# The values of a gated linear attention by seven block products of 512 columns, and weight tiles placed by the step at which they come free

## The chip, the cores and the metric

The kernel runs on one core of a Trainium2 chip. The metric is the device time of one execution in microseconds (us). Before the change three runs gave 1188.12, 1188.62 and 1190.53 us, so the median is 1188.62.

## What is computed

Three residual layers on x of 512 tokens by 1024 features, all in fp32: a gated feed-forward network (FFN) with weight 0.5, a mixer, and a second FFN with weight 0.5; then a last norm.

```python
def swiglu(x, w_gu, w_down):                      # D_FF = 2816
    g, u = jnp.split(x @ w_gu, 2, axis=-1)
    return (jax.nn.silu(g) * u) @ w_down

def hybrid_mixer(h, w_in, ...):                   # 4 heads, dk 128, dv 256, CHUNK 64
    z = h @ w_in
    cb, cc, cu, q, k, v, g_lr, r, ga, gb = jnp.split(z, SPLIT_POINTS, axis=-1)
    y_conv = (cb * causal_short_conv(cc * cu, conv_w)) @ w_out_conv
    log_a = jax.nn.log_sigmoid(g_lr @ gate_w_up + gate_b) / GATE_TAU
    o = gla_chunked(q, k, v, log_a)
    o = o * lax.rsqrt(jnp.mean(o * o, axis=-1, keepdims=True) + EPS)
    y_gla = (o * gla_norm_g * jax.nn.silu(r)) @ w_out_gla
    merged = jax.nn.sigmoid(ga) * y_conv + jax.nn.sigmoid(gb) * y_gla
    return merged @ w_o

def reference(x, ...):
    x = x + 0.5 * swiglu(rmsnorm(x, norm_ffn1_g), ffn1_w_gu, ffn1_w_down)
    x = x + hybrid_mixer(rmsnorm(x, norm_mix_g), w_in, ...)
    x = x + 0.5 * swiglu(rmsnorm(x, norm_ffn2_g), ffn2_w_gu, ffn2_w_down)
    return rmsnorm(x, final_norm_g)
```

For each head and each chunk of 64 tokens, gla_chunked works out scores of q and k under decays, their product with the values v, and a state of 128 x 256 that is carried from chunk to chunk.

## The kernel before, in words

**Three matmuls for each product.** Weights come from HBM as tiles of 128 x 1024 fp32 (512 KB, name f) through SP's DMA queue (line 285). ScalarE (ACT) casts a tile to its high part wh (line 312), VectorE (DVE) forms the low part wl as the difference of tile and cast (line 313). Activations are kept as such pairs too (name op). A product is then wh x op-high + wl x op-high + wh x op-low: three matmuls on TensorE (PE) of 512 or 256 columns each, summed in a bank of 128 x 512 fp32 (names mm and aux).

**Sets of seven products.** Most of the wide products run as sets: a 2 x 2 block product by seven block products instead of eight, named m1, p2, q6, p5, q7, p4, p3. In the sets of 256 columns (line 501) weights are the stationary operand. A set loads four tiles a11, a12, a21, a22. A DVE sum forms s3 = a11 + a21 (line 299), and accumulating DMAs on GpSimd's (POOL's) queue form the other sums in place (line 290): a21 += a22 with the sum s3, a11 += a21 after the cast for m1, a12 += a11 after the cast for p2. The activations' sums are made by a class Operands (make; on DVE, lines 540 to 561, 600 and 737). The FFN's down product begins with two sets in the other layout ("wide", line 799, function run_wide): there the activations are stationary and 512 columns of weights move; each product consists of two half sets of 12 matmuls on two banks.

**What sets the order.** PLAN lists the weight tiles in the order of use and STEPS the casts (a tile alone, or a set and its product). The class Weights goes through STEPS two casts ahead of TensorE: each take issues what is due, that is loads (those of a set six steps ahead of its m1), sums (three steps ahead), the cast and the difference. Each engine works through its instructions in the order in which the program issues them. The f tiles come from a pool that hands out ten buffers in a ring: a new tile waits until the tile that was issued ten tiles ago has been read for the last time.

**The mixer.** First come q and k of heads 0 and 1 (mm_group, line 361), with the low-rank gates beside them. Then come the values, in two halves of 512 columns for heads 0 and 1, and 2 and 3 (v_half, which calls mm_wide, lines 378 to 380): for each pair of weight tiles all four blocks of 128 tokens, on four banks. Between the halves stand q and k of heads 2 and 3 (mm_single, line 347). Behind them come twelve sets (MSETS) for the gates ga and gb, the convolution (conv, cb) and r. The heads' chain (gates, decays, scale, scores, state, output, squares) runs within this order: for head 0 in the first half of the values and the singles, for head 1 from the last single to set 0, for heads 2 and 3 by hooks in sets 1 to 5. The outputs O of heads 0 and 1 are first kept in tiles that the convolution needs and are copied to their own tile after set 0 (move). The values are made from the activations before the norm's factor of each token, so k is multiplied by the factor's square (row2).

## Time and profile before

| | |
|---|---|
| runs | 1188.12, 1188.62, 1190.53 us |
| the profiled execution, its whole time | 1188.83 us |
| its span in the profile | 1187.1 us |
| share of time: PE, DVE, ACT, POOL | 99%, 72%, 53%, 9% |
| HBM | 124.55 MB read, 8.39 MB written |

The span reaches from the first to the last instruction of the profiled execution. Times in rows are in us; a row of a group names line, engine, operation, the tile written and the tiles read, and the count. "mean" durations are from an instruction's start to its end; neighbours on an engine overlap, so the pace of a stage is read from start to start. "Idle before" is time in which the engine had nothing running ahead of the group's instructions, with the engine that ended most of it.

The casts, differences and sums of all stages together:

```profile
L312 ACT CAST wh<-f 128x1024 fp32r<-128x1024 f32 (+1 forms) x335 | 349.5, 1046 | 406.0 <-PE mm L501 226.9
L313 DVE TENSOR_TENSOR wl<-f,wh 128x1024 fp32r<-128x1024 f32 (+1 forms) x335 | 405.9, 1216 | 169.4 <-ACT wh L312 160.0
L501 PE MATMUL mm<-op,wh 128*128 128x256 f32 x3584 | 470.3, 284 | 1.0 <-ACT tp L509 0.9
```

### The profile page before, as it was taken

The page shows a single profiled execution, that of the slowest core. Times are in us where ns is not written, and L with a number is a line of the kernel's source. Part 1 is how long each engine was busy: PE and PEld are TensorE (multiplying, and loading weights), DVE is VectorE, ACT ScalarE, POOL GpSimd, SP SyncE. Part 2 cuts the span into 40 slices and gives each one's busy share as a digit, 9 for nine tenths or more (in the row PEclk, how much of TensorE's full clock was granted, in tenths as well). Part 3 has the DMA queues.
Part 4 walks back from the last instruction along what each step waited for, and adds up shares of the span by engine and source line. Part 5 has one row for each costly group of instructions (what it writes and reads, how often), then busy time and mean ns, then how long its engine had stood idle before and what let it go on. Part 6 is the DMA issues. An engine that isn't in the chain of part 4 may idle for free. (4 is left out here: it accounts for less than half of the span.)

```text
span 1187.1 us, 19179 instructions
## 1 busy us (share of the span) xinstructions
PE 1176.9 (99%) x7818; PEld 1084.1 (91%) x7818; DVE 858.5 (72%) x1016; ACT 629.8 (53%) x784; POOL 111.8 (9%) x147
## 2 busy tenths in 40 slices
PE   9999999999999999999999999999999999999997
PEld 7899999988888889999999998998889999998876
DVE  7986665896578765768577687685598666579955
ACT  6554544675345465656554576544355454556443
POOL 0011111101010001101111100100001111001100
PEclk9999999999999999999999999999999999999999
DMA  9387777678532335867887766542538777757721
GB/s 350 80 219 187 179 187 186 150 198 209 196 112 83 89 71 156 203 192 205 219 230 176 194 195 186 142 125 80 177 76 212 167 186 174 191 142 184 173 87 71
DMA packets 61736, 197.10 MB, mean 166 GB/s; under 512 B 6768, under 2 KB 13040, under 8 KB 61648
## 3 DMA queue, kind: packets, MB, share of 16 engines
q1 hardware_dynamic: 39088, 126.37, 30.4%
q0 software_dynamic: 17920, 65.02, 29.8%
q10 hardware_dynamic: 4640, 4.49, 1.2%
q8 instruction: 61, 1.00, 0.3%
q14 instruction: 27, 0.22, 0.1%
HBM read 124.55 MB, written 8.39 MB: 112 GB/s over the span
## 5 line engine op out<-in xcount | busy, mean ns | idle before, releaser
L312 ACT CAST wh<-f 128x1024 fp32r<-128x1024 f32 (+1 forms) x335 | 349.5, 1046 | 406.0 <-PE mm L501 226.9
L313 DVE TENSOR_TENSOR wl<-f,wh 128x1024 fp32r<-128x1024 f32 (+1 forms) x335 | 405.9, 1216 | 169.4 <-ACT wh L312 160.0
L501 PE MATMUL mm<-op,wh 128*128 128x256 f32 x3584 | 470.3, 284 | 1.0 <-ACT tp L509 0.9
L501 PEld LDWEIGHTS mm<-op,wh 128*128 128x128 f32 x3584 | 447.4, 192 | 2.6 <-ACT tp L509 1.3
L501 PE MATMUL mm<-op,wl 128*128 128x256 f32 x1792 | 251.5, 283 | 0.0
L501 PEld LDWEIGHTS mm<-op,wl 128*128 128x128 f32 x1792 | 231.3, 192 | 0.1
L290 POOL DMA_DIRECT2D f<-f x120 | 103.6, 869 | 927.2 <-DVE wl L313 504.6
L347 PE MATMUL mm<-op,wh 128*128 128x512 f32 x384 | 91.8, 391 | 0.0
L347 PEld LDWEIGHTS mm<-op,wh 128*128 128x128 f32 x384 | 71.9, 188 | 14.8
L799 PE MATMUL mm<-wh,op 128*128 128x512 f32 x320 | 79.2, 390 | 0.1
L799 PEld LDWEIGHTS mm<-wh,op 128*128 128x128 f32 x320 | 59.9, 188 | 12.9 <-ACT wh L312 0.6
L361 PE MATMUL mm<-op,wh 128*128 128x512 f32 x256 | 63.8, 391 | 0.3 <-DVE op L412 0.3
L361 PEld LDWEIGHTS mm<-op,wh 128*128 128x128 f32 x256 | 47.8, 188 | 10.7 <-ACT acc L421 0.5
L299 DVE TENSOR_TENSOR f<-f,f 128x1024 f32<-128x1024 f32 x40 | 48.9, 1221 | 0.7
L347 PE MATMUL mm<-op,wl 128*128 128x512 f32 x192 | 47.4, 389 | 0.0
L347 PEld LDWEIGHTS mm<-op,wl 128*128 128x128 f32 x192 | 36.0, 188 | 7.5
L799 PE MATMUL mm<-wl,op 128*128 128x512 f32 x160 | 42.8, 389 | 0.0
L509 ACT COPY tp<-mm 128x512 f32<-128x512 f32 x68 | 39.7, 583 | 0.0
L799 PEld LDWEIGHTS mm<-wl,op 128*128 128x128 f32 x160 | 30.0, 188 | 6.2
L361 PE MATMUL mm<-op,wl 128*128 128x512 f32 x128 | 34.4, 391 | 0.0
L600 DVE TENSOR_TENSOR op<-hidw,op 128x1024 fp32r<-128x1024 f32 x28 | 33.9, 1218 | 0.1
L415 ACT ACTIVATE op<-X,vec 128x512 fp32r<-128x512 f32 x23 | 16.6, 720 | 31.8 <-DVE X L852 24.3
(273 smaller groups left out, 1151.6 us busy)
## 6 DMA issues: line engine op xcount, KB each, us to landing
f<-wts SPq DMA_DIRECT2D x219, 512.0 KB, 4.4
f<-f POOLq DMA_DIRECT2D x120, 512.0 KB, 4.9
X<-xT SPq DMA_DIRECT2D x8, 256.0 KB, 5.2
xs<-X POOLq DMA_DIRECT2D x8, 256.0 KB, 2.3
ga<-tp ACTq DMA_DIRECT2D x8, 256.0 KB, 2.9
gb<-tp ACTq DMA_DIRECT2D x8, 256.0 KB, 5.0
tp<-ga SPq DMA_DIRECT2D x8, 256.0 KB, 5.2
y<-tp SPq DMA_DIRECT2D x7, 256.0 KB, 2.0
```

What stands on the lines that cost most here:

```text
L290: return nc.gpsimd.dma_start(out_, a, accum_op=ALU.add).ins
L299: nc.vector.tensor_tensor(out=s3, in0=a11, in1=a21, op=ALU.add)
L312: self.cast = nc.scalar.copy(h[:, :w], raw[:, :w]).ins
L313: nc.vector.tensor_tensor(out=l[:, :w], in0=raw[:, :w], in1=h[:, :w].bitcast(F32), op=ALU.subtract)
L347: nc.tensor.matmul(o, w[:, i * P : (i + 1) * P], a[k], start=j == k == 0, stop=j == 2 and k == kt - 1)
L361: nc.tensor.matmul(o[c], w[:, s : s + P], a[k], start=k == 0 and j == 0, stop=k == kt - 1 and j == 2)
L415: nc.scalar.activation(xh[k], x[k], AF.Copy, scale=g)
L501: nc.tensor.matmul(to, ww[:, s], aa[:, t], start=fresh and k == 0 and e == 0 and j == 0, stop=k == 3 and j == 2, skip_group_check=True)
L509: nc.scalar.copy(v, o)
L600: nc.vector.tensor_tensor(out=lv, in0=v, in1=hv.bitcast(F32), op=ALU.subtract)
L799: nc.tensor.matmul(o[t], aa[:, s], ww[:, i * 512 : (i + 1) * 512], start=fresh and j == k == 0, stop=j == 2 and k == 3, skip_group_check=True)
```

## The change

1. **Values.** mm_wide and the list wide are gone. The four singles (q and k of heads 2 and 3) come directly after the first group. Behind them the values of all heads run as one wide set of 1024 columns, by the body of run_wide, which becomes a function (natural_set). The operands are those of the sets behind it (xo). The seven results are combined into the values' tiles vt by v_done. Since the operands now carry the norm's factor, k takes it once.
2. **The heads' chain.** Gates, decays and scale of head 0 are issued between the singles, its scores after the first product m1 of the values. All the rest, for four heads, hangs at sets 0 to 8 (the table chain). MSETS has another order at its start. O is written to its own tile from the start.
3. **Load tiles.** The f tiles get ten slots of one buffer each. A load names the step at which its tile is read for the last time (until), and takes the slot whose present tile is freed at the earliest step. A set asks for a21, a11, a22, the sum's tile and a12 in that order; before, it was a11, a12, a21, a22 and the sum's tile. A first set behind a wide set loads eight steps ahead of its m1 instead of six.

```diff
-MSETS = [("ga", 0), ("gb", 0), ("conv", 0), ("ga", 1), ("conv", 1), ("gb", 1), ("conv", 2),
+MSETS = [("ga", 0), ("gb", 0), ("ga", 1), ("conv", 0), ("gb", 1), ("conv", 1), ("conv", 2),
          ("conv", 3), ("cb", 0), ("cb", 1), ("r", 0), ("r", 1)]
...
+SLOTS = 10
 SEQ = ("m1", "p5", "q6", "p2", "q7", "p3", "p4")
...
     units(group("w_in", KD, (QO, KO, QO + P, KO + P)))
-    units(wide("w_in", KD, VO))
     for h in (2, 3):
         units(single("w_in", KD, QO + h * P))
         units(single("w_in", KD, KO + h * P))
-    units(wide("w_in", KD, VO + 512))
+    wide_sets("w_in", 1, VO)
...
                 if p == "m1":
-                    self.loads.setdefault(max(lo, i - first), []).append(n)
+                    after = STEPS[i - 1][1] is not None and PLAN[STEPS[i - 1][0]][4] > HW
+                    wait = PLAN[n][4] == HW and after
+                    self.loads.setdefault(max(lo, i - (8 if wait else first)), []).append(n)
...
+        def slot(self, until):
+
+            i = min(range(SLOTS), key=lambda j: self.until[j])
+            self.until[i] = until
+            cnt[0] += 1
+            return pools["f"].tile([P, 1024], F32, tag=f"f{i}", name=f"f{cnt[0]}")
...
+        def load_set(self, n):
+
+            a = {p: STEPS.index((n, p)) for p in SEQ}
+            for i in range(self.issued, a["m1"]):
+                if STEPS[i][1] is None and STEPS[i][0] not in self.raw:
+                    self.raw[STEPS[i][0]] = self.dma(STEPS[i][0], i)
+            a21 = self.dma(n + 2, max(a["p5"], a["m1"] + 3))
+            a11 = self.dma(n, a["p2"] + 3)
+            a22 = self.dma(n + 3, a["p4"])
+            s3 = self.slot(a["q7"])
+            a12 = self.dma(n + 1, a["p3"])
+            self.raw[n] = [a11, a12, a21, a22, s3]
...
-                self.raw[n] = [self.dma(n + i) for i in range(4)] + [tile_of("f", [P, 1024])]
+                self.load_set(n)
...
+    def natural_set(ops, banks, done, ahead=1):
+
+        used = {"a"}
+        for at, p in enumerate(SEQ):
+            for q in SEQ[at : at + ahead + 1]:
+                ops.make(q)
...
-        mul(row2, row, row)
...
+        def v_done(p, o):
+            for t in range(2):
+                if p == "m1":
+                    nc.scalar.copy(A[t], o[t])
+                elif p == "p2":
+                    nc.scalar.copy(vt[0][t], o[t])
+                elif p == "p5":
+                    nc.scalar.copy(vt[1][2 + t], o[t])
+                elif p == "q6":
+                    nc.scalar.copy(vt[0][2 + t], o[t])
+                elif p == "q7":
+                    v = vt[1][2 + t]
+                    nc.vector.scalar_tensor_tensor(out=v, in0=o[t], scalar=-1.0, in1=v,
+                                                   op0=ALU.mult, op1=ALU.subtract)
+                elif p == "p3":
+                    v = vt[0][2 + t]
+                    nc.vector.tensor_tensor(out=v, in0=o[t], in1=v, op=ALU.add)
+                else:
+                    nc.scalar.activation(vt[1][t], o[t], AF.Copy, scale=-1.0)
+            if p == "m1":
+                scores(0)
+
+        steps = [lambda: gates(0), decays, lambda: scale(0)]
+        for h in range(2, HEADS):
+            for c, evac in ((QO, evac_q), (KO, evac_k)):
+                o = mm_single("w_in", KD, c + h * P, xh, xl)
+                if steps:
+                    steps.pop(0)()
+                if c == QO:
+                    xo.make("p2" if h == 3 else "m1")
+                elif h == 2:
+                    xo.sum("p5")
+                evac(h, o)
+        A = [MM(), MM()]
+        natural_set(xo, {"a": A, "b": [MM(), MM()], "c": [MM(), MM()]}, v_done)
...
+        chain = [(0, "q6", state, 0), (0, "q7", output, 0), (0, "p3", squares, 0),
+                 (1, "q6", gates, 1), (1, "q7", None, 1), (1, "p4", scale, 1),
+                 (2, "q6", scores, 1), (2, "q7", state, 1), (2, "p4", output, 1),
+                 (3, "q6", squares, 1), (3, "q7", gates, 2), (3, "p3", None, 2),
+                 (4, "q6", scale, 2), (4, "p3", scores, 2), (5, "q6", state, 2),
+                 (5, "p4", output, 2), (5, "p3", squares, 2), (6, "q6", gates, 3),
+                 (6, "q7", None, 3), (6, "p4", scale, 3), (7, "q6", scores, 3),
+                 (7, "q7", state, 3), (7, "p4", output, 3), (8, "q6", squares, 3)]
+        for n, p, f, h in chain:
+            hooks[n, p] = [(lambda f=f, h=h: f(h)) if f else decays]
```

Below, the rows name an engine's instructions in the order of its program: line, operation, the tile written and the tiles read, and the shape; a number behind a name tells tiles of one name apart.

TensorE in the values, before: the first rows of a half (wh_3646 and wl_3647 are the parts of its first pair of weight tiles, op_3345 and op_3346 those of an activation tile, mm_3754 to mm_3757 the banks of the four blocks of tokens).

```order
L378 MATMUL mm_3754<-wh_3646,op_3345 128x512
L379 MATMUL mm_3754<-wl_3647,op_3345 128x512
L380 MATMUL mm_3754<-wh_3646,op_3346 128x512
L378 MATMUL mm_3755<-wh_3646,op_3345 128x512
L379 MATMUL mm_3755<-wl_3647,op_3345 128x512
L380 MATMUL mm_3755<-wh_3646,op_3346 128x512
```

The same engine after the change, where product m1 passes from its first half set (wh_3857, wl_3858) to its second (wh_3905, wl_3906); op_3813 and op_3814 are the operand's two parts. Left out are rows that read like the pair above them.

```order
L625 MATMUL mm_3937<-wl_3858,op_3813 128x512
L625 MATMUL mm_3938<-wl_3858,op_3813 128x512
L625 MATMUL mm_3937<-wh_3905,op_3813 128x512
L625 MATMUL mm_3938<-wh_3905,op_3813 128x512
...
L625 MATMUL mm_3937<-wh_3905,op_3814 128x512
L625 MATMUL mm_3938<-wh_3905,op_3814 128x512
...
L625 MATMUL mm_3937<-wl_3906,op_3813 128x512
L625 MATMUL mm_3938<-wl_3906,op_3813 128x512
```

Before, a pair's difference was needed by the pair's second matmul and was used on four banks (48 matmuls for every two pairs). Now a half set has 12 matmuls on two banks, and its difference is needed by the ninth.

VectorE ahead of the values' second half set, after the change: wl_3906 is the difference named above, the rows with g, y and sm scale head 0, L1043 works on the residual X, L1019 evacuates the last but one single product.

```order
L476 TENSOR_TENSOR y_3465<-g_566_3765,y_3465 128x512
L476 TENSOR_TENSOR g_565_3764<-g_565_3764,y_3465 128x4x64
L476 TENSOR_TENSOR g_566_3765<-g_565_3764,y_3465 128x256
L476 TENSOR_TENSOR g_566_3765<-y_3465,sm 128x256
L476 TENSOR_TENSOR y_3465<-g_564_3763,y_3465 128x512
L476 TENSOR_TENSOR g_565_3764<-g_566_3765,sm 128x4x64
L476 TENSOR_TENSOR g_567_3766<-g_566_3765,sm 128x4x64
L476 TENSOR_TENSOR g_567_3766<-y_3465,sm 128x4x64
L476 TENSOR_TENSOR d_3768<-sm 128x4
L1043 SCALAR_TENSOR_TENSOR X<-X,vec,row_3716 128x512 x4
L1019 SCALAR_TENSOR_TENSOR qk_3470<-mm_3856,row_3716 128x512
L332 TENSOR_TENSOR wl_3906<-f_3599,wh_3905 128x1024
```

Before, this scaling stood within the first half of the values, ahead of a difference that only the singles used:

```order
L475 TENSOR_TENSOR y_3465<-g_555_3747,y_3465 128x512
L475 TENSOR_TENSOR g_556_3748<-g_557_3749,sm 128x4x64
L475 TENSOR_TENSOR g_558_3750<-g_557_3749,sm 128x4x64
L475 TENSOR_TENSOR g_558_3750<-y_3465,sm 128x4x64
L313 TENSOR_TENSOR wl_3875<-f_3758,wh_3874 128x1024
L561 TENSOR_TENSOR op_4117<-X,op_4116 128x1024
L540 TENSOR_TENSOR X<-X 128x4x256
```

VectorE in the up product of the second FFN, before: the sum f_10088 of a set (line 299; f_10080 is the set's a11) and the differences behind it, up to the one that reads f_10080 for the set's m1.

```order
L299 TENSOR_TENSOR f_10088<-f_10080,f_10084 128x1024
L710 SCALAR_TENSOR_TENSOR hidw_8771<-mm_9889,tp_9980 128x2x256
L313 TENSOR_TENSOR wl_10185<-f_9848,wh_10184 128x1024
L313 TENSOR_TENSOR wl_10215<-f_9852,wh_10214 128x1024
L715 TENSOR_TENSOR tp_10242<-mm_10050,tp_10048 128x512
L313 TENSOR_TENSOR wl_10253<-f_9856,wh_10252 128x1024
L475 TENSOR_TENSOR hidw_8771<-tp_10119,tp_10242 128x2x256
L313 TENSOR_TENSOR wl_10284<-f_10080,wh_10283 128x1024
```

The same place after the change (the set's a11 is f_10092):

```order
L318 TENSOR_TENSOR f_10096<-f_10092,f_10090 128x1024
L332 TENSOR_TENSOR wl_10133<-f_9865,wh_10132 128x1024
L730 SCALAR_TENSOR_TENSOR tp_10129<-mm_10060,tp_10127 128x512
L332 TENSOR_TENSOR wl_10164<-f_9633,wh_10163 128x1024
L734 SCALAR_TENSOR_TENSOR hidw_8781<-mm_9899,tp_9990 128x2x256
L332 TENSOR_TENSOR wl_10195<-f_9860,wh_10194 128x1024
L332 TENSOR_TENSOR wl_10225<-f_9858,wh_10224 128x1024
L739 TENSOR_TENSOR tp_10252<-mm_10060,tp_10058 128x512
L332 TENSOR_TENSOR wl_10263<-f_9864,wh_10262 128x1024
L476 TENSOR_TENSOR hidw_8781<-tp_10129,tp_10252 128x2x256
L332 TENSOR_TENSOR wl_10294<-f_10092,wh_10293 128x1024
```

Three differences stood between the sum and the set's first one; now there are five.

More of the change, by code (lines that the diff above doesn't have):

```diff
@@ L604, in get @@
             return self.parts[p]
+    def natural_set(ops, banks, done, ahead=1):
[3 more added lines that the diff above has]
+                ops.make(q)
+            n = {"m1": "b", "p2": "a", "q6": "b", "p5": "c", "q7": "b", "p4": "b", "p3": "c"}[p]
+            fresh = n not in used
+            used.add(n)
+            o = banks[n]
+            bh, bl = ops.get(p)
+            for u in range(2):
+                h, l = W.take()
+                for j, (ww, aa) in enumerate(((h, bh), (h, bl), (l, bh))):
+                    for i in range(2):
+                        k = 2 * u + i
+                        for t in range(2):
+                            s = slice(k * HW + t * P, k * HW + (t + 1) * P)
+                            nc.tensor.matmul(o[t], aa[:, s], ww[:, i * 512 : (i + 1) * 512],
+                                             start=fresh and j == k == 0,
+                                             stop=j == 2 and k == 3, skip_group_check=True)
+            done(p, o)
     def run_sets(make, ahead=2, hooks={}):
```

118 lines of the change are left out of this document (21 added, 97 removed).

## Prediction

> **What bounds the kernel now.** I read the page's engine table first, then TensorE's waits, then windows of the stages that the change touches.
>
> ```profile
> span 1187.1 us, 19179 instructions
> PE 1176.9 (99%) x7818; PEld 1084.1 (91%) x7818; DVE 858.5 (72%) x1016; ACT 629.8 (53%) x784; POOL 111.8 (9%) x147
> PEclk9999999999999999999999999999999999999999
> PE aux L228 <- POOL ones L225: 1.1, 1, 1.1
> PE mm L501 <- ACT tp L509: 0.9, 2, 0.5
> PE aux L831 <- DVE X L774: 0.8, 1, 0.8
> ```
>
> TensorE (PE) is busy for 1176.9 of 1187.1 us at full clock, and the list of its waits holds nothing over 1.1 us. A busy PE need not run at its peak, so I check its pace in the stage that is rewritten, the values (lines 378 to 380).
>
> ```profile
> 370.26 0.39 PE L378 MATMUL mm<-wh,op 128*128 128x512 f32 x1
> 375.70 0.40 PE L1065 MATMUL aux<-glr,gup_w 96*128 96x512 f32 x1
> 392.27 3.79 PE L347 MATMUL mm<-op,wh 128*128 128x512 f32 x16
> 422.30 0.40 PE L378 MATMUL mm<-wh,op 128*128 128x512 f32 x1
> 444.13 2.08 PE L501 MATMUL mm<-op,wh 128*128 128x256 f32 x16
> 1069.43 10.01 PE mm L799 x44
> ```
>
> The first half of the values starts at 370.26 and is followed by the next matmul at 392.27; one gate matmul (375.70, next start 375.93) lies in it. That is 22.01 - 0.23 = 21.78 us for its 96 matmuls. The second half runs from 422.30 to 444.13, 21.83 us for 96. Together 43.61 us for 192, or 0.2271 us from start to start. The down product (line 799), which already has the form that the values get, takes 10.01 us for 44, or 0.2275 us. So the stage is bound by TensorE issuing matmuls without a break: removing matmuls there shortens the run, as long as VectorE (DVE) and ScalarE (ACT) still deliver operands in time.
>
> **The change, part by part.**
>
> *Fewer matmuls.* 192 matmuls of 512 columns become 7 products x 2 half sets x 12 = 168. The rows of TensorE's program in the section on the change show the new grouping, and nothing else is added to or taken from TensorE. The price is 24 x 0.2271 = **5.45 us less**. The Trainium skill, page "TensorE: Matmul & The Clock Gate", section "Wait — 56ns, not 53.3ns?", gives 215.7 ns from start to start for 512 columns at full clock; by that the term would be an estimated 5.2 us. The trace has 227 ns for the very instructions removed, so I keep 5.45.
>
> *More casts and differences.* Eight weight tiles become 14 half-set passes, so six casts on ACT and six differences on DVE are added (the wl rows below), and two sums of tiles on DVE and six accumulating DMAs on GpSimd's queue (POOL) come with them.
>
> ```profile
> L313 DVE TENSOR_TENSOR wl<-f,wh 128x1024 fp32r<-128x1024 f32 x333 | 404.5, 1220 | 165.1 <-ACT wh L312 155.7 <-PE aux L831 4.2 <-PE aux L445 4.2
> 396.92 1.22 DVE L561 TENSOR_TENSOR op<-X,op 128x1024 fp32r<-128x1024 f32 x1
> 398.06 1.22 DVE L299 TENSOR_TENSOR f<-f,f 128x1024 f32<-128x1024 f32 x1
> 370.53 0.68 DVE L475 TENSOR_TENSOR tp<-aux,row 96x512 f32<-96x512 f32 x1
> 371.13 0.68 DVE L1014 SCALAR_TENSOR_TENSOR y<-mm,row 128x512 f32<-128x512 f32 x1
> 374.29 2.73 DVE L1039 SCALAR_TENSOR_TENSOR X<-X,vec,row 128x512 f32<-128x512 f32 x4
> 387.90 0.69 DVE L475 TENSOR_TENSOR y<-g,y 128x512 f32<-128x512 f32 x1
> 391.12 1.22 DVE L313 TENSOR_TENSOR wl<-f,wh 128x1024 fp32r<-128x1024 f32 x1
> 370.26:392.27 22.01, 22.01 (x98) 18.21 (x97) 20.88 (x33) 14.88 (x20) 0.00 (x0) 1.00 0.21 72
> 392.27:422.30 30.03, 30.03 (x153) 25.01 (x152) 18.32 (x22) 10.37 (x14) 1.09 (x3) 1.00 0.32 88
> 422.30:444.10 21.80, 21.80 (x97) 18.02 (x96) 17.21 (x25) 14.22 (x19) 1.73 (x2) 1.00 0.31 67
> ```
>
> From start to start a DVE pass over 1024 columns takes 1.14 us, one over 512 takes 0.60 (370.53 to 371.13), a step on X 0.68 (four in 2.73), and the scaling of one head 3.2 (387.90 to 391.12). In the three windows (columns: busy PE, weight loads, DVE, ACT, POOL) DVE was busy 20.88 + 18.32 + 17.21 = 56.4 of 73.8 us, 76%. Into the same stretch, now 68.4 us long, come six differences, two sums less the one that was there, three operand parts (q7, p4, p3) and four combinations of banks: about 6 x 1.14 + 1.14 + 3 x 1.14 + 4 x 0.6 = 13.8 us. Out of it go head 1's gates, decays and scaling (about 2.4 + 1.2 + 3.2) and what head 0 still has to do after its scores (about 3.8), 10.6 us; the second row of norms, 0.68 us, goes as well. That is some 59 of 68.4 us, 86%. TensorE's time hides it on average; ACT, at 39.5 of 73.8 us, has more room. Nothing is charged for the passes themselves; they cost where one comes late.
>
> *The one tight place.* The DVE rows in the section on the change show it: all of head 0's scaling, four steps on X and one evacuation stand ahead of the difference wl_3906, which the second half of product m1 needs. TensorE starts the four single products at 370.26, as it now starts the values, so they end at 370.26 + 4 x 24 x 0.2271 + 0.23 = 392.3. The first half of m1 takes 12 x 0.2271 = 2.73 us, and the second half needs the difference after eight matmuls, 1.82 us on: at 396.8. DVE begins its evacuations at 369.33 and has until there nine passes of 512 columns (5.4), seven steps on X (4.8), eight passes of 1024 columns (four differences, one sum, one operand, p5's subtraction and the scan: 9.1), four short passes of gates and decays (2.4) and the scaling (3.2): 24.9 us, so 394.2 without waits.
>
> ```profile
> 369.33 0.69 DVE L1014 SCALAR_TENSOR_TENSOR y<-mm,row 128x512 f32<-128x512 f32 x1 [0.66 <-PE mm L361]
> DVE g L1073 <- ACT g L1072: 5.9, 4, 1.9
> 1050.00:1100.00 50.00, 49.61 (x293) 44.12 (x293) 45.03 (x46) 32.95 (x37) 6.05 (x7) 1.00 0.69 177
> 1100.00:1150.00 50.00, 49.05 (x214) 39.42 (x213) 43.97 (x46) 25.08 (x25) 5.19 (x6) 1.00 0.56 139
> ```
>
> In a head's gates DVE waited for ACT's logarithm 5.9 us in four heads, at most 1.9 each, so wl_3906 comes at 395.7 to 396.1: in time by less than a microsecond. What a stage at this load costs I read from the down product's windows, with the same code and DVE 90% and 88% busy: TensorE idle 0.39 and 0.95 us in 50. For 41 us of values (38.2 of products, 2.9 of scores) that is 0.3 to 0.8. I take **+0.6 us**, in its upper half, as the tight place lies at the stage's start; the ends are 0 (all in time) and +2.5 (DVE late by two waits for ACT).
>
> *What moves behind.* Heads 1 to 3 ran beside sets 0 to 5, now heads 0 to 3 beside sets 0 to 8.
>
> ```profile
> 500.00:600.00 100.00, 100.00 (x809) 97.61 (x808) 67.80 (x85) 54.98 (x74) 10.35 (x12) 1.00 0.81 218
> 600.00:660.00 60.00, 60.00 (x503) 60.00 (x502) 46.83 (x58) 30.40 (x38) 7.75 (x9) 1.00 0.75 186
> ```
>
> With chain and convolutions DVE was at 68% and 78% there and TensorE never idle. The 10.6 us that arrive spread over three more sets of 7 x 24 x 0.119 = 20 us each (503 matmuls in 60 us give 0.119). A convolution set with the chain then holds roughly 14 + 5 us of DVE in 22 us of TensorE, 86%: below the down product's load. I charge 0, with 0 to +1 for the range. Between m1 and the end of the chain its matmuls are the same ones, only later.
>
> *Loads by order of release.* A tile's slot is now the one freed earliest, and a set's first two loads are those that its sum needs.
>
> ```profile
> f<-wts SPq DMA_DIRECT2D x219, 512.0 KB, 4.4
> L290 POOL DMA_DIRECT2D f<-f x120: 851/860/1212, 26.3 to 1124.7; - x120
> DMA to landing us min/median/max: 4.5/4.9/7.7
> 1128.17 4.62 DMA f<-wts
> 1133.77 1.06 ACT wh L312
> 1147.67 0.61 DVE X L774
> 1148.32 0.50 PE aux L831
> 1128.00:1150.00 22.00, 21.05 (x90) 16.25 (x89) 16.13 (x17) 11.82 (x12) 0.00 (x0) 1.00 0.38 116
> ```
>
> A load takes 4.4 us and an accumulation 4.9, mostly hidden: TensorE's idle time above has only one place where a load stands in the chain that ended last, the last block of the kernel, where one issued at 1128.17 holds back ACT and, through DVE's passes until 1148, 0.95 us of TensorE in 22. Two of the loads of that block still queue behind the same accumulation in the new order, and ACT still takes late tiles ahead of casts of the set. I charge 0; the ends are -1.3 (this place and the 0.39 at 1050 gone) and +0.7 (one more difference late there, 1.14 less the half that is covered). For the six accumulations added, the second half of product q6 is the nearest to its need: issued after wl_3906 at 396, landing by 403.7 with the longest of 7.7 us, needed at 408.8.
>
> [...]
>
> *Sum.* 1188.83 (the profiled execution, span 1187.1 and 1.7 around it) - 5.45 + 0.6 = 1183.98. The median of the runs shown, 1188.62, is 0.2 lower, so the forecast in its terms is **1183.8**; the cases below are in the same terms. A measurement of this kernel tells about 0.2% (2.4 us) from no change.
>
> **Rivals.**
>
> *VectorE falls behind at the start of the values.* For it speaks the margin of under 1 us at wl_3906; against it that every later difference has 3 us or more, since scores (2.9 us of TensorE without weights from DVE) follow m1. Each microsecond past 396.8 is a microsecond of TensorE. With 2 us more than I take: 1185.8.
>
> *The loads also free the last block.* For it speaks that the wait of 0.95 us begins with a load held by its ring place. Against it the queue and cast order just named. With 1.3 us gone and 0.4 of the values' waits: 1188.6 - 5.45 - 1.3 + 0.2 = 1182.1.
>
> *Sums ahead of their loads (slower).* In 22 sets of 256 columns the sum of two tiles now stands five differences ahead of the set's first one in DVE's order, where most had three (rows in the section on the change). DVE takes its work in order, so a sum whose load has not landed holds all differences behind it. By the plan's numbers a slot is free three products, 3 x 2.86 = 8.6 us, before the sum; a load of 4.4 us fits, an accumulation of 4.9 and a load behind it, 9.3, do not. From there on each set would lose the excess, 0.7 us, of which two differences in hand hide about half: with 22 such sets 22 x 0.35 = 8 us, so 1192. Against it: DVE waited 0.7 us in all before its 40 sums so far, and loads and accumulations share the queues in parallel.
>
> ```profile
> L299 DVE TENSOR_TENSOR f<-f,f 128x1024 f32<-128x1024 f32 x40 | 48.9, 1221 | 0.7
> ```
>
> That the matmuls are not saved cannot be: the program lists them.
>
> **Chances and range.** Forecast 0.55 (its own range 1182.6 to 1185.2), VectorE late 0.18 (1184.8 to 1187.3), last block freed 0.20 (1181 to 1182.6), sums held up 0.07 (1187.5 to 1195). The range 1181.2 to 1187.0 leaves out the slower case and the edges of the others. Faster than 1186.2: 0.55 + 0.20 + 0.12 = 0.87; within 0.2%: 0.06 + 0.02 = 0.08; above 1191.0: 0.05.
>
> **What would show it.** In the changed profile the values take 168 matmuls at 0.227 us with no start-to-start gap above 1 us at the second half of m1; a gap there, with a DVE difference as releaser, is the first rival. TensorE's idle time at 1128 to 1150, shifted by 5 us, stays near 0.95 or goes (second rival). DVE's idle time before the sums stays near 1 us in all; tens of microseconds there would be the third. I am wrong if TensorE is idle in the sets with convolutions, or if a 512-column matmul of the values takes other than 0.227 us.

## The result and the profile after

| | time, us | against before | 95% interval |
|---|---|---|---|
| before, first comparison | 1189.0 (4 runs) | | |
| changed | 1182.24 (4 runs, 1180.99 to 1182.82) | 0.9943 | 0.9931 to 0.9955 |
| changed, run again in a later comparison | 1181.22 (5 runs) against 1189.15 (21 runs) | 0.9933 | 0.9921 to 0.9946 |

The kernel is 6.8 us faster, 7.9 in the later comparison; the forecast was 4.8 less than 1188.62. The profiled execution took 1180.99 us, the fastest of the first four. Its page answers the lines shown before the change like this (the engine table, and the chain that ended last by engine):

```profile
span 1179.3 us, 19168 instructions
PE 1170.9 (99%) x7794; PEld 1080.7 (92%) x7794; DVE 868.9 (74%) x1027; ACT 634.3 (54%) x790; POOL 117.4 (10%) x153
PE 97%; ACT 1%; issue 1%; DVE 1%; ACTq 0%; POOL 0%; POOLq 0%
```

The chain of work that ended last is now TensorE's own program for 97% of the span: it leads through no load and no accumulation any more. On the page before, the part of the chain that could be followed covered 12% of the span, and 2% of it were transfers. TensorE's waits (us in all, times, longest):

```profile
PE aux L224 <- POOL ones L221: 1.1, 1, 1.1
PE mm L502 <- ACT mm L507: 0.4, 2, 0.2
```

The windows of the two stages that had idle time, and of the values (columns as before):

```profile
1042.00:1092.00 50.00, 50.00 (x306) 45.05 (x305) 46.41 (x47) 33.28 (x37) 5.23 (x6) 1.00 0.67 179
1092.00:1142.00 50.00, 50.00 (x221) 41.06 (x220) 43.83 (x46) 26.40 (x26) 5.17 (x6) 1.00 0.58 147
392.27:433.50 41.23, 41.23 (x189) 33.87 (x188) 36.65 (x37) 23.88 (x29) 5.27 (x7) 1.00 0.69 175
```

The two windows (the same stages as 1050 to 1150 before, 8 us earlier) hold no idle time where 0.39 and 0.95 us stood. What is left of TensorE's waits behind the values are two of 0.2 us in the sets, where the kernel before has one. In the values TensorE is busy throughout although VectorE is busy for 36.65 of 41.23 us, 89%. VectorE's sums, in the list of groups, still wait for next to nothing:

```profile
L318 DVE TENSOR_TENSOR f<-f,f 128x1024 f32<-128x1024 f32 x42 | 51.3, 1222 | 0.8
```

Now the tight place, in the timeline of TensorE and of VectorE (start, duration, instruction):

```profile
392.29 1.98 PE L625 MATMUL mm<-wh,op 128*128 128x512 f32 x8
395.01 1.98 PE L625 MATMUL mm<-wh,op 128*128 128x512 f32 x8
396.82 1.07 PE L625 MATMUL mm<-wl,op 128*128 128x512 f32 x4
433.40 2.08 PE L502 MATMUL mm<-op,wh 128*128 128x256 f32 x16
395.18 1.22 DVE L332 TENSOR_TENSOR wl<-f,wh 128x1024 fp32r<-128x1024 f32 x1
```

The difference is done at 395.18 + 1.22 = 396.40, and TensorE takes it at 396.82 without a break: a margin of 0.4 us. The values with head 0's scores take 433.40 - 392.29 = 41.1 us, as forecast (38.2 + 2.9).

### The profile page after: what moved, and what is told of

Its sections match the earlier page's. It is cut to its first block, busy times and chain, and to the rows that moved or that the text cites. A ratio compares the mean times of both kernels' runs of the same rounds, so it can differ in the third digit from the quotient of the medians.

```text
span 1179.3 us, 19168 instructions
## 1 busy us (share of the span) xinstructions
PE 1170.9 (99%) x7794; PEld 1080.7 (92%) x7794; DVE 868.9 (74%) x1027; ACT 634.3 (54%) x790; POOL 117.4 (10%) x153
## 4 chain that ended last, share of the span: by engine, by line
PE 97%; ACT 1%; issue 1%; DVE 1%; ACTq 0%; POOL 0%; POOLq 0%
PE mm L502 53%; PE mm L625 12%; PE mm L366 11%; PE mm L380 7%; PE mm L838 4%; PE aux L625 4%; PE aux L838 1%; PE aux L1161 1%; PE aux L1142 1%; PE aux L1120 1%; PE aux L1164 0%; PE aux L224 0%; PE aux L1121 0%; PE mm L857 0%; PE aux L771 0%
## 5 line engine op out<-in xcount | busy, mean ns | idle before, releaser
L331 ACT CAST wh<-f 128x1024 fp32r<-128x1024 f32 (+1 forms) x341 | 356.2, 1047 | 406.3 <-PE mm L502 207.4
L332 DVE TENSOR_TENSOR wl<-f,wh 128x1024 fp32r<-128x1024 f32 (+1 forms) x341 | 413.3, 1217 | 154.1 <-ACT wh L331 141.3
L309 POOL DMA_DIRECT2D f<-f x126 | 108.9, 869 | 929.0 <-DVE wl L332 542.2
L625 PE MATMUL mm<-wh,op 128*128 128x512 f32 x432 | 106.9, 389 | 0.0
L625 PEld LDWEIGHTS mm<-wh,op 128*128 128x128 f32 x432 | 80.9, 188 | 16.7
L625 PE MATMUL mm<-wl,op 128*128 128x512 f32 x216 | 57.7, 389 | 0.0
L318 DVE TENSOR_TENSOR f<-f,f 128x1024 f32<-128x1024 f32 x42 | 51.3, 1222 | 0.8
L625 PEld LDWEIGHTS mm<-wl,op 128*128 128x128 f32 x216 | 40.6, 188 | 8.4
```

Source lines behind the costliest of these rows:

```text
L309: return nc.gpsimd.dma_start(out_, a, accum_op=ALU.add).ins
L318: nc.vector.tensor_tensor(out=s3, in0=a11, in1=a21, op=ALU.add)
L331: self.cast = nc.scalar.copy(h[:, :w], raw[:, :w]).ins
L332: nc.vector.tensor_tensor(out=l[:, :w], in0=raw[:, :w], in1=h[:, :w].bitcast(F32), op=ALU.subtract)
L625: nc.tensor.matmul(o[t], aa[:, s], ww[:, i * 512 : (i + 1) * 512], start=fresh and j == k == 0, stop=j == 2 and k == 3, skip_group_check=True)
```

## The experiments

Twelve kernels were run in three comparisons; each row is against the kernel before in its own comparison. "Gaps" are TensorE's waits in the one profiled execution, beyond the small ones that the changed kernel has too. The changed kernel itself was run in the first comparison (in the section above) and in the last, so a run of another comparison is set against it by the ratios to the kernel before.

| run | time, us | ratio to before, interval | what its profile shows |
|---|---|---|---|
| set, ring, old load order | 1184.93 | 0.9966, 0.9954 to 0.9978 | gaps in m1, the first set, the end |
| old values, slots | 1187.98 | 0.9994, 0.9986 to 1.0003 | gaps of before stay |
| slots, old load order | 1193.55 | 1.0037, 1.0025 to 1.0048 | sums wait for loads |
| six steps ahead, not eight | 1181.47 | 0.9935, 0.9923 to 0.9948 | none |
| 2 passes more ahead of m1's second half | 1182.89 | 0.9952, 0.9940 to 0.9965 | a gap there, two of 0.5 us elsewhere |
| 6 passes more | 1185.05 | 0.9971, 0.9961 to 0.9981 | three gaps, a halved clock for 3.4 us |
| 24 matmuls less | 1179.90 | 0.9922, 0.9910 to 0.9935 | a gap in the first set, a halved clock for 3.4 us |
| set, ring, new load order | 1183.43 | 0.9956, 0.9942 to 0.9970 | gaps in m1, the first set, the end |
| 24 matmuls more | 1188.30 | 0.9993, 0.9984 to 1.0002 | two gaps of before are back |
| old order of sets | 1180.97 | 0.9932, 0.9920 to 0.9945 | one of 0.3 us |
| before again | 1189.04 | 0.9998, 0.9989 to 1.0007 | two of three gaps |
| changed again | 1181.22 | 0.9933, 0.9921 to 0.9946 | none |

### Which part gives what

**The values' set with the ring and the load order of before.** The class Weights is that of before, so the first set behind the values loads six steps ahead, and the pools are f=10:

```diff
-                self.load_set(n)
+                self.raw[n] = [self.dma(n + i) for i in range(4)] + [tile_of("f", [P, 1024])]
```

> The values by the set of seven products and the chain behind it, but load tiles in the ring of ten and in the order of before, six steps ahead. Theory: the matmuls give 24 x 0.227 = 5.45 us and the slots the other 2 us or so, by freeing the end of the last down product; so about 5.4 us less than before, and TensorE's wait of about 0.95 us ahead of the late units of the down product is back, with 1.5 to 1.9 us of gaps there in all. Rival A: with the ring, the first 256-column set behind the values gets its tiles too late (each waits for a tile of the values' set that is cast late): gaps of 1 to 3 us in the first set, 3 to 5 us less than before. Rival B: the gaps at the end went for another reason than the slots: they are absent here too, and the time is that of the changed kernel, about 7 us less than before.

It is 4.1 us below before, between the theory and rival A. TensorE's waits in its profile:

```profile
PE mm L479 <- ACT tp L487: 1.6, 1, 1.6
PE aux L815 <- DVE X L775: 0.8, 1, 0.8
PE mm L602 <- DVE wl L309: 0.6, 1, 0.6
```

Three waits are there that the changed kernel does not have. The first (L479) is rival A in place and size. The chain of waits in the first set leads back to an accumulation; that a late load stands behind it, as rival A has it, the chain doesn't show:

```profile
432.50 6.85 DMA f<-f
...
441.41 0.49 ACT tp L487
```

An accumulation issued at 432.50 lands 6.85 us later; ACT's casts wait for it, and the evacuation that TensorE needs stands behind them. The second wait is the end of the down product, as the theory had it. The third, at the second half of m1, is the prediction's first rival. VectorE's timeline at the start of the values:

```profile
375.16 1.22 DVE L295 TENSOR_TENSOR f<-f,f 128x1024 f32<-128x1024 f32 x1
382.51 1.22 DVE L295 TENSOR_TENSOR f<-f,f 128x1024 f32<-128x1024 f32 x1
396.50 1.22 DVE L309 TENSOR_TENSOR wl<-f,wh 128x1024 fp32r<-128x1024 f32 x1
```

Here both sums of the values' half sets (375.16, 382.51) stand between VectorE's first evacuation of q and k at 369.5 and the tight difference, which starts at 396.50, 1.3 us later than in the changed kernel. There only one sum (374.98) stands in that stretch; the other is done at 354.24, ahead of it. A pass of 1024 columns is 1.14 us. So the set alone saves its 5.45 us and gives about 1.4 back.

**The slots with the old values.** The kernel before with the new class Weights and ten pools of one buffer:

```diff
-                self.raw[n] = [self.dma(n + i) for i in range(4)] + [tile_of("f", [P, 1024])]
+                self.load_set(n)
```

> The kernel before with the slots and the new load order alone; values and chain as before. Theory: TensorE's gaps at the end of the last down product (1.9 us in all, 0.95 the longest) and at the ends of the two set stretches (0.65 and 0.55) go, all 216 matmuls of the values and singles stay: 2 us less than before. Rival: the gaps stay, 0 to 0.4 us less.

It gave 0.7 us by the ratio, and the interval reaches no change. The theory fell: the waits of before are still there.

```profile
PE mm L525 <- ACT tp L533: 1.7, 2, 1.0
PE aux L855 <- DVE X L798: 0.7, 1, 0.7
```

The slots alone give little; with the set they take away what the set would otherwise give back. -4.1 and -0.7 make -4.8, both together -6.8 or -7.9. In time this difference of 2 to 3 us is hardly wider than the intervals; what shows it are the waits of the set's run that the changed kernel doesn't have. The end of the down product needs the set and the slots: with the slots alone its wait of 0.7 us stays.

**The old order of a set's loads, with slots.**

```diff
-            a21 = self.dma(n + 2, max(a["p5"], a["m1"] + 3))
             a11 = self.dma(n, a["p2"] + 3)
+            a12 = self.dma(n + 1, a["p3"])
+            a21 = self.dma(n + 2, max(a["p5"], a["m1"] + 3))
             a22 = self.dma(n + 3, a["p4"])
             s3 = self.slot(a["q7"])
-            a12 = self.dma(n + 1, a["p3"])
```

> The changed kernel, but each set asks for its tiles in the old order (a11, a12, a21, a22, then the sum's tile), with the slots kept. Theory: what frees the end of the down product is the choice of the slot, so that a unit's load no longer waits for an accumulation; the order within a set only moves loads by one another: within 0.5 us of the changed kernel, no gap over 0.3 us at the end. Rival: the order does it, since the accumulation a21 += a22 starts once a21 and a22 are there, one load earlier: the gaps at the end are back and the time is 1 to 2 us above the changed kernel.

Both were wrong: it is slower than before, and over 11 us slower than the changed kernel. VectorE's sums in the list of groups:

```profile
L318 DVE TENSOR_TENSOR f<-f,f 128x1024 f32<-128x1024 f32 x42 | 51.4, 1223 | 9.9 <-DMA f<-wts 7.3 <-issue 1.9
```

One of them in the timeline (in brackets the idle time before it):

```profile
261.05 1.23 DVE L318 TENSOR_TENSOR f<-f,f 128x1024 f32<-128x1024 f32 x1 [2.66 <-DMA f<-wts]
```

What TensorE waited for:

```profile
PE mm L502 <- ACT tp L510: 3.2, 2, 2.9
```

This is the prediction's third rival, brought about by the order of the requests. VectorE waited 9.9 us ahead of its 42 sums where the changed kernel has 0.8, and all differences stood behind. TensorE's list of waits adds up to 7.9 us here and to 1.5 in the changed kernel; the two profiles differ by 10 us, and the rest stays open. By the code, each request takes the slot that comes free next: in the old order a12, needed last of all, takes an early one, and a21, needed by the sum, a late one. A placement by order of release needs requests in order of need.

**The ring with the new load order.**

```diff
-                self.raw[n] = [self.dma(n + i) for i in range(4)] + [tile_of("f", [P, 1024])]
+                a21, a11, a22 = (self.dma(n + i) for i in (2, 0, 3))
+                s3 = tile_of("f", [P, 1024])
+                self.raw[n] = [a11, self.dma(n + 1), a21, a22, s3]
```

> The values by the set with load tiles in the ring of ten, but each set's loads in the new order (a21, a11, a22, the sum's tile, a12). Against the run with the ring and the old order, which had gaps of 1.7 us in the first set behind the values and of 0.8 us at the second half of m1. Theory: the ring place, not the order, made those loads late, so the 1.7 us stay (in the ring the new order gives a21 the place that was a11's) and the time is within 0.7 us of that run. Rival: the order is what counts; both gaps go, and the time is that of the changed kernel within 0.7 us.

TensorE's waits:

```profile
PE aux L817 <- DVE X L777: 0.7, 1, 0.7
PE mm L604 <- DVE wl L311: 0.6, 1, 0.6
PE mm L481 <- ACT tp L489: 0.5, 1, 0.5
```

The wait in the first set fell from 1.6 to 0.5 us, so that part was the order's. The one at m1 (0.6) stayed, and with slots and the same six steps it is absent (run below), so it belongs to the ring. The one at the end of the down product stayed too; the run before this one has it with slots and the old order (0.7), so it goes only with both. In time (5.2 us below before, against 4.1 with the old order) the two intervals overlap.

**Six steps ahead, and the old order of the sets.**

```diff
-                    self.loads.setdefault(max(lo, i - (8 if wait else first)), []).append(n)
+                    self.loads.setdefault(max(lo, i - first), []).append(n)
```

> The changed kernel, but the first 256-column set behind the values loads six steps ahead of its m1, not eight. Theory: two casts in hand (some 5 us) hide the later loads: the same as the changed kernel within 0.5 us. Rival: q6 of that set waits for two accumulations in a row behind a late load: a gap of 1 to 3 us on TensorE in the first set, and as much more time.

```diff
-MSETS = [("ga", 0), ("gb", 0), ("ga", 1), ("conv", 0), ("gb", 1), ("conv", 1), ("conv", 2),
+MSETS = [("ga", 0), ("gb", 0), ("conv", 0), ("ga", 1), ("conv", 1), ("gb", 1), ("conv", 2),
```

> The changed kernel with the first convolution set back in third place (the old order of the sets), where VectorE has head 1's scores, state and output too. Theory: with 86% of VectorE's time taken there at most, TensorE's time hides it: within 0.5 us of the changed kernel, no new gap over 0.3 us in sets 0 to 8. Rival: convolution and chain together are more than a set's 20 to 22 us of TensorE, and gaps of 1 to 3 us appear in the third set.

Neither made a difference that can be measured (1181.47 and 1180.97, the changed kernel 1182.24 and 1181.22). With the old order TensorE has one new wait of 0.3 us, for VectorE in the heads' chain. The window of the first eight sets with the old order:

```profile
433.50:600.00 166.50, 165.99 (x1343) 162.44 (x1342) 113.88 (x145) 99.14 (x135) 18.43 (x24) 1.00 0.74 187
```

TensorE is idle for 0.5 us in it, in the changed kernel for 0.4. VectorE is 68% busy there (113.88), so what moved behind the values is covered in either order.

### The tight place and the price of a matmul

**Two and six passes more ahead of m1's second half.**

```diff
-        steps = [lambda: gates(0), decays, lambda: scale(0)]
+        def extra():
+            junk = T()
+            for _ in range(2):
+                mul(junk, row, row)
+
+        steps = [lambda: gates(0), decays, lambda: (scale(0), extra())]
```

> The changed kernel with two idle VectorE passes of 512 columns (a product written to a scratch tile that nothing reads) behind head 0's scaling, 1.2 us ahead of the difference that the second half of product m1 needs. In the changed kernel that difference ended at 396.40 and TensorE took it at 396.82. Theory: nothing ahead of it can absorb the passes (VectorE waits for nothing between the scaling and it), so the margin of 0.4 us is used up and TensorE shows one gap of about 0.8 us at the ninth matmul of that half; 0.8 us more than the changed kernel. Rival: casts and differences in hand hide it, no gap.

TensorE's timeline (in brackets the idle time before):

```profile
397.61 1.20 PE L625 MATMUL mm<-wl,op 128*128 128x512 f32 x4 [0.67 <-DVE wl L332]
```

The matmuls that need the difference started at 397.61 instead of 396.82, after waiting for it: 0.8 us, as expected from the margin of 0.4. In time it is 1.1 to 2.3 us (ratio 0.9952 against 0.9943 and 0.9933, with intervals that overlap); a wait of 0.5 us in the first set and one of 0.5 at the end of the down product came with it. Some of VectorE's instructions behind the difference stand in another order here too.

> The same with six such passes, 3.6 us. Theory: past the margin each microsecond counts in full, one gap of about 3.2 us at the same matmul and 3.2 us more than the changed kernel; the products behind are not later by more than that, since TensorE is late too. Rival A: lookahead hides part of it, a gap of 1 to 2 us. Rival B: VectorE, 89% busy in the values, cannot catch up with what it still has to do for the products behind m1, further gaps follow and the loss is 4 us or more.

TensorE's waits:

```profile
PE mm L625 <- DVE wl L332: 1.2, 1, 1.2
PE mm L625 <- ACT wh L331: 1.0, 1, 1.0
PE mm L502 <- ACT tp L510: 0.9, 1, 0.9
```

It lost 3.3 to 4.5 us. The profile shows three waits instead of one, and something that the list of waits doesn't hold: the clock granted to TensorE (as a share of full speed) was 0.50 from 402.0 to 405.2, right behind the first wait. The 12 matmuls from 401.52 on took 4.45 us where 12 at 0.227 take 2.73, so it cost another 1.7 us. The program's order is not the same: the instructions are placed by a scheduler, which has put head 0's scores ahead of the four matmuls that need the late difference, and some casts and differences in another order. So the wait at m1 is shorter than expected, and the next two are new. What the two runs show is that lateness past 0.4 us costs there; how much of the larger delay is paid at m1 alone was not separated.

**24 matmuls less, and 24 more,** in products q7, p3 and p4 of the values.

```diff
+                last = 1 if short and p in ("q7", "p3", "p4") else 2
-                for j, (ww, aa) in enumerate(((h, bh), (h, bl), (l, bh))):
+                for j, (ww, aa) in enumerate(((h, bh), (h, bl), (l, bh))[: last + 1]):
```

> The changed kernel without the 24 matmuls of the weights' low part in products q7, p3 and p4 of the values (8 each; their differences are still made), so these three products leave out that part of the result. Theory: TensorE bounds the values, each matmul is worth 0.227 us, so 5.4 us less than the changed kernel, and no new gap. Rival: VectorE is the bound behind it. It was busy 36.65 of 41.23 us in this stretch, and has 35.8 us now; gaps of 1 to 2.5 us appear in the values or the first set, and the gain is 3 to 4.5 us.

The gain over the changed kernel is 1.3 to 2.5 us (ratio 0.9922 against 0.9933 and 0.9943, with intervals that overlap), less than both said. The values themselves got shorter as the theory has it: set 0 starts 35.67 us behind the first matmul of the values, 5.44 less than in the changed kernel. The rest was lost behind them. TensorE has one new wait, of 2.5 us, in its timeline (in brackets):

```profile
436.94 3.51 PE L502 MATMUL mm<-op,wh 128*128 128x256 f32 x16 [2.50 <-ACT tp L510]
```

The window behind it (columns as before; the last three are the granted clock, the DMA engines' share and GB/s):

```profile
437.40:440.60 3.20, 3.20 (x17) 3.20 (x16) 2.99 (x4) 1.45 (x3) 0.00 (x0) 0.50 0.76 145
```

The chain that ends in that wait:

```profile
429.52 5.75 DMA f<-f
...
436.94 0.39 PE mm L502
```

The first set's sum in VectorE's timeline:

```profile
427.85 1.22 DVE L318 TENSOR_TENSOR f<-f,f 128x1024 f32<-128x1024 f32 x1
```

Two losses follow. An accumulation of the first 256-column set, issued at 429.52 and landing 5.75 us later, held ACT's cast and the evacuation behind it: 2.5 us. That accumulation had waited for VectorE's sum of the same set, which starts at 427.85; in the changed kernel it starts at 424.94, although TensorE comes to the set 5 us later there. VectorE worked without a break from 421.89 on, where the changed kernel leaves it idle for 1.7 us in two places, so the rival's bound is at work. But the scheduler has also put two differences and the two combinations for product p3 ahead of the sum, some 3.5 us of passes, so how much of the 2.5 us a fixed order would have stays open. The second loss is again the granted clock, 0.50 for 3.4 us from 437.3 on (the window above lies within): the 24 matmuls from 436.94 on took 4.47 us, the 24 from 428.53 on 2.87, so 1.6 us. 5.44 - 2.5 - 1.6 leaves 1.3. The five runs spread from 1177.32 to 1180.18 us; the mean granted clock was 0.997 in three of them, the profiled one among them, and 0.999 in the two fastest.

```diff
+                more = twice and p in ("q7", "p3", "p4")
+                parts = ((h, bh), (h, bl), (l, bh)) + (((l, bh),) if more else ())
-                for j, (ww, aa) in enumerate(((h, bh), (h, bl), (l, bh))):
+                for j, (ww, aa) in enumerate(parts):
```

> The changed kernel with 24 matmuls more in the values: in products q7, p3 and p4 the weights' low part is multiplied twice (so this part counts double in the result). The other engines do the same work. Theory: a 512-column matmul of the values is worth 0.227 us as long as nothing else makes TensorE wait; the changed kernel has no gap there, so 5.4 us more, 1187.3 to 1188.0. Rival: something else paces the values by then (VectorE, at 89%, or the loads of the first set), and part of the added time only fills waits: 3 to 4.5 us more.

The first matmul of the values and the first of set 0 in TensorE's timeline:

```profile
392.37 0.84 PE L627 MATMUL mm<-wh,op 128*128 128x512 f32 x3
438.92 2.08 PE L502 MATMUL mm<-op,wh 128*128 128x256 f32 x16
```

From the first matmul of the values to the first of set 0 it took 438.92 - 392.37 = 46.55 us, in the changed kernel 41.11: 5.44 us for 24 matmuls, 0.227 each, the theory to the hundredth. The whole run is 7.1 us above the changed kernel of the same comparison, though: a wait of 1.2 us appeared at 790, where the kernel before has one too, and one of 0.2 at the end of the down product. The first set's new waits of the three runs above are absent here, where TensorE comes to the set later and its operands don't.

### The wait at 790

**The kernel before, and the changed one, once more,** without an edit.

> The kernel before once more, to see whether its gaps belong to it. Theory: the gaps at the ends of the two stretches of sets (0.65 and 0.55 us) and at the end of the last down product (0.95) come from its schedule of loads and accumulations and return, each within a factor of two; the accumulation ahead of the first two takes over 5.1 us again. Rival: they are chance, and one or more of them is gone in this execution.

> The changed kernel once more. Theory: none of the three gaps is there, the accumulations ahead of the first two take under 4.9 us, TensorE's gaps are as few as in the first profile, and the time is 6 to 7.5 us below the kernel before. Rival: at least one of the gaps returns, and the part of the gain beyond the 24 matmuls is chance: 5 to 6 us below the kernel before.

In the kernel before, the wait at the end of the mixer's last sets is back (1.3 us here) and that at the end of the down product (0.8); that in the second FFN's sets (0.55) is not. The changed kernel has none of the three again. For the wait at 790, GpSimd's accumulation a12 += a11 of the last set and ACT's cast that waits for it, in the timeline, first of the kernel before, then of the changed one:

```profile
783.88 0.87 POOL L290 DMA_DIRECT2D f<-f  x1 [16.75 <-DVE wl L313]
790.08 1.05 ACT L312 CAST wh<-f 128x1024 fp32r<-128x1024 f32 x1 [4.34 <-DMA f<-f]
```

```profile
779.17 0.86 POOL L309 DMA_DIRECT2D f<-f  x1 [16.75 <-DVE wl L332]
784.02 1.05 ACT L331 CAST wh<-f 128x1024 fp32r<-128x1024 f32 x1 [2.99 <-DMA f<-f]
```

From issue to cast it is 6.2 us in one and 4.85 in the other; the difference is TensorE's wait. The DMA view of just these stretches (queues, then transfers with their time to landing), of the kernel before and of the changed one:

```profile
q8 instruction: 1, 0.02, 1.7%
...
f<-f POOLq DMA_DIRECT2D x1, 512.0 KB, 6.1
```

```profile
q0 software_dynamic: 144, 0.52, 61.4%
q1 hardware_dynamic: 47, 0.18, 13.3%
f<-f POOLq DMA_DIRECT2D x1, 512.0 KB, 4.7
```

A transfer of instructions (16 KB on queue 8, one of 61 in a run) falls into the accumulation in the first and not in the second. In all fourteen profiles: in the four with TensorE's old count of matmuls (before twice, the slots with old values, 24 more) it does, and the accumulation took 5.29 to 6.10 us; in the ten with fewer it does not, and it took 4.74 to 4.79. A load of 512 KB shares the stretch in all fourteen, issued 2.2 us behind the accumulation, so its being there doesn't make the difference. 61 transfers of 16 KB are 1.0 MB, or 64 bytes for each of TensorE's 15,600 matmuls and weight loads, and between two of them lie 256 of these on average: they are TensorE's own program, so that 24 matmuls (48 instructions) fewer ahead of this place move where they fall. The Trainium skill, page "Runtime: NRT & Kernel Launch", section "Instruction fetch mechanics", has the same blocks (16 KiB, 256 instructions) and calls the cost mostly hidden. In these traces it is 0.5 to 1.4 us of one accumulation, and not hidden where the next product waits for it.

The wait of 0.39 us at 1063 before the change is of the same kind. In TensorE's timeline:

```profile
1063.41 2.18 PE L501 MATMUL mm<-op,wh 128*128 128x256 f32 x16 [0.39 <-ACT tp L509]
```

The accumulation in the chain that ends there:

```profile
1056.11 5.62 DMA f<-f
```

A transfer of instructions falls into this accumulation in the same four runs, 0.4 to 1.8 us behind its issue. In three of them it took 5.18 to 5.62 us, and two of these have the wait; in the kernel before, run once more, it took 4.66 with the transfer inside, and the wait is absent. In the ten others such a transfer comes 4.3 us behind the issue or not at all, the accumulation took 4.5 to 4.9 us, and there is no wait. So a transfer inside lengthens an accumulation often, not always. That it is the cause is concluded from its coming and going with the delay in these profiles; it was not moved by itself.

## Why the prediction was right, and where it was off

- **Fewer matmuls, -5.45 us: right.** The values take the 41.1 us that 168 matmuls at 0.227 us and 2.9 of scores make, and 24 matmuls more or less changed them by 5.44 us either way.
- **The one tight place, +0.6: not paid.** The working had the difference at 395.7 to 396.1 and its need at 396.8; it came at 396.4. The step that failed is reading the stage's cost from the down product's idle time. With 0.4 us left nothing is lost, and that idle time was not of "the same code": the 0.39 us stands at 1063.41, in a set of 256 columns ahead of the down product (line 501), and 0.79 of the 0.95 at 1148.32, in the units behind its wide sets (line 831). The wide sets lost less than 0.2 us in all, with VectorE busy for 97% of their first 30 us:

```profile
1069.50:1100.00 30.50, 30.50 (x136) 25.25 (x135) 29.45 (x30) 20.28 (x23) 2.61 (x4) 1.00 0.79 202
```

  The first rival is real beyond the margin: the ring (0.6 us) and the two passes more (0.8 us) show it.
- **What moves behind, 0: right within a fraction.** The sets have one new wait of 0.2 us, with the old order of the sets one of 0.3; the prediction's band was 0 to 1.
- **Loads by order of release, 0: mis-sized; it was -0.95.** This is the second rival, and the measured time lies in its band (1181 to 1182.6) rather than in the forecast's own (1182.6 to 1185.2). But of the rival's 1.3 us only the 0.95 of the last block belong to the loads. The other 0.39 is the wait at 1063, which is also absent in the kernel before when run again and in both runs with the ring, so that part of the hit was luck. "Two of the loads of that block still queue behind the same accumulation" holds for two of four. Before, all four did, by two waits on two accumulations; now the other two wait for a difference. What SP's queue waited for in that block, before and after:

```profile
SPq L285 <- DMA f<-f: 11.7, 2, 10.4
```

```profile
SPq L291 <- DMA f<-f: 9.9, 1, 9.9
SPq L291 <- DVE wl L332: 3.1, 3, 2.3
```

  The gain there is thin: with slots and the new order the gap is absent in six profiles and 0.2 to 0.7 us by the list of waits in three (two passes more, 24 more, old values), while with the ring it is 0.7 to 0.8 in all four.
- **Sums ahead of their loads: right not to expect, and rightly named.** The new load order prevents it; without that the run is 11 to 12 us longer, more than the 8 that the rival was given.
- **Not seen:** about half a microsecond at 790 (1.3 in the second pair of profiles), which goes with where TensorE's instruction blocks fall and not with the slots or the sets as such.

Together: -5.45 for the matmuls, -0.95 for the last block, -0.39 at 1063, about -0.5 at 790 and about -0.4 in two short breaks between matmuls of the old singles (0.19 each, from start to start) make -7.7 of the -7.8 us between the two profiled executions (1188.83 and 1180.99). The medians differ by 6.8 and 7.9. So the forecast of 1183.8 was 1.6 above the first median (1182.24) and 2.6 above the second (1181.22), which is at the very edge of the range 1181.2 to 1187.0: about 1 us of it from the last block, 0.6 from the tight place, and what is left from waits that no term of the sum held.

## What to carry to other kernels

Where an engine is busy for 99%, count its instructions at the stage's own start-to-start pace; that part of a forecast holds to a per cent, and what is left to judge is which waits come and go. A change of the bound engine's work can open waits that a change of the loads' placement closes, so the two can be worth more together (here -6.8 or -7.9 us) than apart (-4.1 and -0.7), though the intervals leave little of this difference certain. Idle time of a window is worth looking up instruction by instruction before it is taken as the price of a stage. A run that comes out slower than its waits explain deserves a look at the granted clock of the windows behind its longest wait. And a placement that hands out what comes free next must be asked in the order of need: the same slots with the old order of requests made this kernel slower than before.

## What was not expected of the hardware

- The transfers that bring TensorE's own instructions fall into the weights' transfers: one 512 KB accumulation took 5.3 to 6.1 us with such a transfer inside it and 4.7 to 4.8 without. Adding or taking away matmuls moves where they fall, and a wait came and went with that 380 us later. That one causes the other is likely, not shown.
- Behind two waits, of 2.5 us (24 matmuls less) and 1.2 us (six passes more), the granted clock went to 0.50 for 3.4 us, from 0.4 us behind the wait's end on, and cost 1.6 to 1.7 us more. Waits of 2.9 us (slots, old load order) and 1.6 us (set, ring, old load order) had no such drop, so what sets it off stays open here.
- VectorE at 89% for 41 us, with ACT at 58% beside it (23.88 of 41.23), did not cost TensorE a single wait in the changed kernel's values.
